# Landing two quarters of the first modulation's weights in empty weight slots, and taking the first products one stage later

## The chip, the core and the metric

The kernel runs on one core of a Trainium2 chip. The time is the device's, in microseconds (us), from the start of the program to its end; the kernel before took 2618.04 us (median of three runs, 2617.7 to 2619.2). A core has TensorE (PE in the profile; PEld is its loading of the stationary operand), VectorE (DVE), ScalarE (ACT), GpSimd (POOL) and SyncE (SP). Each works through its own list of instructions in the order in which the program gives them, and they wait for each other and for transfers by semaphores. SP issues nearly all transfers from the chip's memory (HBM) into SBUF; PSUM is what TensorE writes.

## The reference, cut to what matters

A diffusion block of two layers over 256 rows of x and 256 of a context, then four layers over x. The change touches the beginning of the first layer alone, for `i = 0`:

```python
m_lat = (jax.nn.silu(c) @ ada_w[i] + ada_b[i])[:, None, :]
m_ctx = jax.nn.silu(c_ctx) @ ada_w[i] + ada_b[i]
sh1, sc1, g1, sh2, sc2, g2 = jnp.split(m_lat, 6, axis=-1)
h  = _rms(x, norm1_g[i]) * (1.0 + sc1) + sh1          # (1, 256, 1024)
hc = _rms(y, norm1_g[i]) * (1.0 + csc1) + csh1        # the context, the same way
# first lines of the even mixer: h @ ev_w_in, hc @ ev_w_in, 1280 columns:
# 512 of the Fourier part (f0, f1), 512 of q (q0, q1), 256 of k and v (kv)
```

So a vector of 1024 is multiplied by 1024 x 2048 weights (shift and scale, 8 MB), x and the context are normalised, scaled and shifted by the result, and these are multiplied by 1024 x 1280 weights (five units of 256 columns, 1 MB each).

## The kernel before, in words

**Precision.** Products with large weights are done as three matmuls of a short form: a weight unit `wraw` of 128 x 2048 f32 is split into a high part `whi` (a cast on ScalarE) and a low part `wlo` (a subtraction on VectorE), each in two halves of 1024; activations are split the same way into `hTh` and `hTl`. One product (`mm3`) is whi x hTh, wlo x hTh, whi x hTl. The modulation's weights are not split: `wraw` is multiplied by `silu_c` as it is.

**Weights.** The class `Weights` keeps one list of units in the order of use. `load` (L249) takes the next unit, a free raw buffer of three (`RAW_BUFS`), and lets SP issue the transfer; the modulation's units are issued in two pieces of 512 KB (L258), others in one of 1 MB (L260). `split` (L286) takes a free weight slot, a pair of `hi` and `lo` buffers, and emits the two casts and two subtractions. At the start there are three slots, "0", "1" and "2". `pump` (L265) does both as far as buffers allow, and is called whenever a unit is done with (`done`, L322) and at each poll. Whether a split is emitted at such a point is decided by the class `Pace`, a running account of when each engine would be free. The order of instructions is so fixed when the program is built; which splits, softmax steps and products stand before which follows from that account, and everything in the first layer's attention is placed by it too. Its numbers are its own; the times in this text are the trace's.

**The first modulation.** `Even.plan` (L1631) puts the 2048 columns into four quarters p = 0..3 of 256 columns of the shift and 256 of the scale, two units (h = 0, 1) of 1 MB each, with the first three units of the mixer behind the first three quarters: ada0, f0, ada1, kv, ada2, q0, ada3. `Even.start` (L1649) loops over p: the two units are multiplied by `silu_c` into a bank (`acc<-wraw,silu_c`); VectorE copies the bank out (`rows`); TensorE transposes the four pieces (`acc<-consts,rows`); VectorE reduces them (`red`) and makes shift `sh` and scale `sc`; both engines apply them to columns 2p and 2p + 1 of the transposed x (`hf<-xT,sh,sc`); a cast and a subtraction give `hTh` and `hTl` of these columns. Products are put between: those of f0 up to column 2p ahead of the transposition of the rows, those of kv and q0 behind it (`products(1, 2 * p)`, `products(p, 2 * p)`). The context is loaded and normalised (`bins[1].A`) in the stage p = 2. After the loop the context's first 128 rows are transposed (`acc<-consts,hn`), the last products of f0, kv and q0 are taken, and the results are copied out by ScalarE (`f<-mm`, `kv<-mm`, `q<-acc`). The second 128 rows' transposition (`mm<-consts,hn`) writes banks that were f0's.

Almost all instructions pass one helper, so they have the line L67; they are told apart by the names of their tiles.

Of the kernel before, what the change touches and what calls it, by code (L numbers as in the profile page):

```python
# [7 lines left out]
F32 = mybir.dt.float32  # L8
F32R = mybir.dt.float32r
# [6 lines left out]
KD = 8  # L16
# [40 lines left out]
class Engine:  # L57


    def __init__(self, eng, name, pace):  # L60
        self.eng, self.name, self.pace = eng, name, pace
# [150 lines left out]
class Weights:  # L212
# [5 lines left out]
    def __init__(self, K):  # L218
        self.K = K
        self.units = []  # L220
        self.index = {}
        self.dma_n = self.split_n = 0
        self.at = -1
        self.part = None
        self.finished = set()
        self.raw = {}
        self.hl = {}
        self.raw_free = list(range(RAW_BUFS))
        self.slots = []
        self.closing = set()  # L230

# [14 lines left out]
    def check_closed(self, name):  # L246
        assert all(x[2][1] != name for x in self.hl.values()), name

    def load(self):  # L249
        key, src, raw, _ = self.units[self.dma_n]  # L250
        nc = self.K.nc
        r = self.raw_free.pop(0)
        t = self.K.raw_p.tile([128, 2048], F32, tag=f"raw{r}", name="wraw")
        shp = src.shape
        if len(shp) == 4:
            v = t.rearrange("p (a b c) -> p a b c", a=shp[1], b=shp[2])
            for i in range(shp[2]):
                nc.sync.dma_start(out=v[:, :, i, :], in_=src[:, :, i, :])  # L258
        else:
            nc.sync.dma_start(out=t if len(shp) == 2 else t.rearrange("p (a b) -> p a b", a=shp[1]), in_=src)  # L260
        nc.loaded(t)
        self.raw[self.dma_n] = (t, r)
        self.dma_n += 1

    def pump(self, force=None):  # L265
        now = self.K.nc.now
        while True:
            moved = False
            if self.dma_n < len(self.units) and self.raw_free:
                self.load()  # L270
                moved = True
            if self.split_n < self.dma_n:
                u = self.split_n
                ahead = sum(not x[2] for x in self.units[self.at + 1:u])
                lead = SPLIT_LEAD[min(ahead, len(SPLIT_LEAD) - 1)]
                idle = max(now["act"], now["dve"]) <= self.K.t + lead and (ahead < HOLD_AHEAD or not self.K.soon())
                if self.units[u][2]:
                    self.split_n += 1
                    moved = True
                elif force is not None and u <= force or \  # L280
                        idle and self.K.nc.ready(self.raw[u][0]) <= max(self.K.t, now["act"]) + 200:
                    moved = self.split(u)
            if not moved:
                return
# [37 lines left out]
    def done(self, key, need=3):  # L322
        u = self.index[key]
        self.finished.add(u)
        if self.units[u][2]:
            self.raw_free.append(self.raw.pop(u)[1])
        if u in self.hl:
            slot = self.hl.pop(u)[2]
            if slot[1] not in self.closing:
                self.slots.append(slot)  # L330
        self.K.poll(need)


class Kernel:
# [52 lines left out]

    @staticmethod
    def slot(pool):
        return lambda tag: pool.tile([128, 2048 + 128], F32R, tag=tag, name="w" + tag[:2])  # L390

    def close_ext(self, n):
        if n in self.ext:
# [803 lines left out]
class Conv:  # L1197
    PADL = 15
    W = 288
# [423 lines left out]
class Even:  # L1623
# [7 lines left out]
    def plan(self):  # L1631
        K = self.K
        w = K.a["ada_w"][0]
        for p in range(4):
            for h in range(2):
                src = w[h * 512:h * 512 + 512, 0:2048].rearrange("(k p) (x n) -> p k x n", p=128, x=2)
                K.W.add(("ada0", p, h), src[:, :, :, p * 256:p * 256 + 256], raw=True)
            if p < 3:
                K.add_in(("e", self.UNITS[p][0]), K.a["ev_w_in"][0], self.UNITS[p][1], "nat")
        for n, c in self.UNITS[3:]:  # L1640
            K.add_in(("e", n), K.a["ev_w_in"][0], c, "nat")
        for g in (1, 2):
            for k in range(KD):
                K.ada_plan(0, g, k)
        for e in range(2):
            for i in range(4):
                K.add_down(("e", "d", e, i), K.a["ev_w_out"][0], i)

    def start(self, bins):  # L1649


        K, nc, W = self.K, self.K.nc, self.K.W
# [3 lines left out]
        hT = bins[0].hT = K.new_hT()  # L1656
# [1 line left out]
        K.mod[0, "sh1"], K.mod[0, "sc1"] = sh, sc  # L1658
        bias, gain = K.sp("ab").rearrange("p (x k) -> p x k", x=2), K.sp("n1")
        far = K.acct()  # L1660
        units, done, xT = [], [0, 0, 0], []
        for p in range(4):
            for h in range(2):
                w = W.get(("ada0", p, h))
                for j in range(4):
                    K.mm32(far[0][32 * j:32 * j + 32, :], K.silu_c[:, 4 * h + j, :], w[:, j * 512:j * 512 + 512], h == 0, h == 1,
                           share=4, tile_position=(0, 32 * j))
                W.done(("ada0", p, h))
            if p == 2:
                for t in range(2):  # L1670
                    nc.sync.dma_start(out=K.y[t], in_=K.a["ctx"][0, t * 128:t * 128 + 128, :])
                    nc.loaded(K.y[t])
                    bins[1].A(t)
            rows = K.ada_p.tile([128, 512], F32, tag="r0", name="rows")
            nc.vector.tensor_copy(rows, far[0])
            if p == 0:
                for t in range(2):
                    ps = K.transposed(bins[0].h[t])
                    xT.append(K.h1_p.tile([128, KD, 128], F32, tag="h1", name="xT", bufs=2))
                    for b in range(2):  # L1680
                        (nc.vector.tensor_copy if b else nc.scalar.copy)(xT[t][:, 4 * b:4 * b + 4, :], ps[b])
                two = K.acct()
                units = [[K.mmt([128, 256]) for _ in range(2)] for _ in range(2)] + [[x[:, 0:256] for x in two]]

            def products(n, k1):
                for i in range(n):
                    wh, wl = W.get(("e", self.UNITS[i][0]))
                    for t in range(2):
                        s = slice(t * 128, t * 128 + 128)
                        for k in range(done[i], k1):  # L1690
                            K.mm3(units[i][t], hT[0][:, k, s], hT[1][:, k, s], wh[:, k, :], wl[:, k, :], k == 0, k == KD - 1)
                    done[i] = k1
                    K.tick()
            if p:
                products(1, 2 * p)
            tp = far[1].rearrange("p (c n) -> p c n", c=4)
            for c in range(4):
                K.tr(tp[:, c, :], rows[:, c * 128:c * 128 + 128])
            red = K.ada_p.tile([128, 2, 2, 2], F32, tag="red", name="red", bufs=2)
            nc.vector.tensor_reduce(out=red, in_=tp.rearrange("p c (j r) -> p c r j", j=4)[:, :, 0:2, :], axis=mybir.AxisListType.X, op=ALU.add)  # L1700
            if p:
                products(p, 2 * p)
            f = slice(2 * p, 2 * p + 2)
            bc = lambda x: x[:, f].unsqueeze(2).to_broadcast([128, 2, 2])
            out = lambda x: x[:, :, f].rearrange("p e k -> p k e")
            nc.vector.tensor_tensor(out=out(sh), in0=red[:, 0], in1=bc(bias[:, 0]), op=ALU.add)
            nc.vector.tensor_tensor(out=red[:, 1], in0=red[:, 1], in1=bc(bias[:, 1]), op=ALU.add)
            nc.vector.scalar_tensor_tensor(out=out(sc), in0=red[:, 1], scalar=1.0, in1=bc(gain), op0=ALU.add, op1=ALU.mult)
            hf = (K.s4_p if p % 2 else K.h1_p).tile([128, 2, 256], F32, tag=("hf", "junk")[p % 2], name="hf", bufs=1)
            for k in (2 * p, 2 * p + 1):  # L1710
                x = k - 2 * p
                nc.scalar.activation(out=hf[:, x, 0:128], in_=xT[0][:, k, :], func=AF.Identity, scale=sc[:, 0, k:k + 1], bias=sh[:, 0, k:k + 1])
                nc.vector.tensor_scalar(out=hf[:, x, 128:256], in0=xT[1][:, k, :], scalar1=sc[:, 0, k:k + 1], scalar2=sh[:, 0, k:k + 1],
                                        op0=ALU.mult, op1=ALU.add)
            K.split_psum(hT[0][:, f, :], hT[1][:, f, :], hf)

        bins[1].finish(0)
        halves = K.transposed(bins[1].h[0], [x.rearrange("p (j c) -> p j c", j=4) for x in far])
        products(3, KD)
        bins[1].hT = K.new_hT(1)  # L1720
        K.transpose_h(halves, bins[1].hT, 0, bins[1].cols())
        bins[1].put_off(1)
# [671 lines left out]
```

## Time and profile before

| | |
|---|---|
| median of three runs | 2618.04 us (2617.7 to 2619.2) |
| the profiled execution | 2618.8 us, span 2617.0 us |
| TensorE busy | 2539.5 us, 97% of the span |
| VectorE, ScalarE busy | 1494.3 us (57%), 1201.8 us (46%) |
| transfers | 453.59 MB, mean 173 GB/s |
| granted TensorE clock, mean | 0.993 of full speed |

The granted clock is a share of 2.4 GHz; 0.5 is 1.2 GHz. Engines work at the same time, so busy times don't add up to the span. In a timeline a row is a group of like instructions: start, busy time, engine, line, operation, output<-input, count, and in brackets the idle time of the engine ahead of it and what ended that.

### The profile page before, as it was taken

The page shows a single profiled execution, that of the slowest core. Times are in us where ns is not written, and L with a number is a line of the kernel's source. Part 1 is how long each engine was busy: PE and PEld are TensorE (multiplying, and loading weights), DVE is VectorE, ACT ScalarE, POOL GpSimd, SP SyncE. Part 2 cuts the span into 40 slices and gives each one's busy share as a digit, 9 for nine tenths or more (in the row PEclk, how much of TensorE's full clock was granted, in tenths as well). Part 3 has the DMA queues.
Part 4 walks back from the last instruction along what each step waited for, and adds up shares of the span by engine and source line. Part 5 has one row for each costly group of instructions (what it writes and reads, how often), then busy time and mean ns, then how long its engine had stood idle before and what let it go on. Part 6 is the DMA issues. An engine that isn't in the chain of part 4 may idle for free.

```text
span 2617.0 us, 43849 instructions
## 1 busy us (share of the span) xinstructions
PE 2539.5 (97%) x18444; PEld 2264.1 (87%) x18444; DVE 1494.3 (57%) x2420; ACT 1201.8 (46%) x2050; POOL 117.2 (4%) x168
## 2 busy tenths in 40 slices
PE   7889999999999999999999899999999999999998
PEld 5648877788877999999998689989998999999998
DVE  4477333366666655756555465555655655755644
ACT  4555222245444544545444354445554544544542
POOL 1100000001221000000000000000000000000000
PEclk9999999999999999999999999999999999999999
DMA  7355454545453655554655726544343654554652
GB/s 266 119 204 193 144 196 162 190 149 165 128 175 109 227 194 202 177 177 146 216 197 175 219 97 210 194 168 155 130 145 105 217 193 167 182 201 145 211 193 88
DMA packets 320741, 453.59 MB, mean 173 GB/s; under 512 B 20760, under 2 KB 281112, under 8 KB 315424
## 3 DMA queue, kind: packets, MB, share of 16 engines
q1 hardware_dynamic: 315552, 434.63, 49.9%
q0 software_dynamic: 4128, 14.11, 1.5%
q8 instruction: 145, 2.38, 0.4%
q10 hardware_dynamic: 864, 2.05, 0.2%
q14 instruction: 52, 0.43, 0.0%
HBM read 448.48 MB, written 2.28 MB: 172 GB/s over the span
## 4 chain that ended last, share of the span: by engine, by line
PE 84%; DVE 7%; DMA 4%; ACT 3%; issue 1%; SPq 1%; POOL 1%; POOLq 0%; DVEq 0%; ACTq 0%
PE mm L67 61%; PE acc L67 23%; DVE wlo L67 2%; DMA u<-up 1%; DMA wraw<-ada_w 1%; DVE sm L67 1%; DVE hTl L67 1%; DVE hn L67 1%; POOL ny L67 1%; ACT whi L67 1%; ACT jk L67 1%; ACT sm L67 0%; ACT hTh L67 0%; DMA wraw<-od_w_in 0%; SPq L1991 0%
## 5 line engine op out<-in xcount | busy, mean ns | idle before, releaser
L67 DVE TENSOR_TENSOR wlo<-wraw,whi 128x1024 fp32r<-128x1024 f32 x592 | 700.5, 1223 | 371.3 <-ACT whi L67 370.2
L67 ACT CAST whi<-wraw 128x1024 fp32r<-128x1024 f32 x592 | 592.7, 1048 | 311.3 <-issue 172.4
L67 PE MATMUL mm<-hTh,whi 128*128 128x256 f32 (+1 forms) x1840 | 543.1, 295 | 1.8 <-ACT hTh L67 1.8
L67 PE MATMUL mm<-hTl,whi 128*128 128x256 f32 (+1 forms) x1840 | 541.6, 294 | 0.3 <-DVE hTl L67 0.3
L67 PE MATMUL mm<-hTh,wlo 128*128 128x256 f32 (+1 forms) x1840 | 541.7, 294 | 0.0
L67 PE MATMUL mm<-whi,hTh 128*128 128x256 f32 x1616 | 464.5, 287 | 5.1 <-ACT hTh L67 3.2
L67 PE MATMUL mm<-whi,hTl 128*128 128x256 f32 x1616 | 455.2, 282 | 5.9 <-DVE hTl L67 5.9
L67 PE MATMUL mm<-wlo,hTh 128*128 128x256 f32 x1616 | 456.2, 282 | 0.9 <-DVE wlo L67 0.9
L67 PEld LDWEIGHTS mm<-hTh,whi 128*128 128x128 f32 x1840 | 346.1, 188 | 15.8 <-ACT hTh L67 2.0
L67 PEld LDWEIGHTS mm<-hTl,whi 128*128 128x128 f32 x1840 | 346.2, 188 | 13.1 <-DVE hTl L67 0.5
L67 PEld LDWEIGHTS mm<-hTh,wlo 128*128 128x128 f32 x1840 | 346.1, 188 | 11.2
L67 PEld LDWEIGHTS mm<-whi,hTh 128*128 128x128 f32 x1616 | 305.5, 189 | 23.1 <-issue 9.7
L67 PEld LDWEIGHTS mm<-whi,hTl 128*128 128x128 f32 x1616 | 307.7, 190 | 8.0 <-DVE hTl L67 8.0
L67 PEld LDWEIGHTS mm<-wlo,hTh 128*128 128x128 f32 x1616 | 306.5, 190 | 1.6 <-DVE wlo L67 1.1
L67 PE MATMUL acc<-whi,ckh 128*128 128x512 f32 x664 | 261.4, 394 | 0.0
L67 PE MATMUL acc<-whi,ckl 128*128 128x512 f32 x664 | 258.6, 390 | 0.6 <-DVE ckl L67 0.6
L67 PE MATMUL acc<-wlo,ckh 128*128 128x512 f32 x664 | 259.1, 390 | 0.0
L67 PE MATMUL mm<-hTh 128*128 128x256 f32 x656 | 184.6, 281 | 0.5 <-ACT hTh L67 0.5
L67 PE MATMUL mm<-hTh,hTl 128*128 128x256 f32 x656 | 182.9, 279 | 0.4 <-DVE hTl L67 0.4
L67 PE MATMUL mm<-hTl,hTh 128*128 128x256 f32 x656 | 182.9, 279 | 0.0
L67 DVE TENSOR_TENSOR hTl<-wraw,hTh 128x1024 fp32r<-128x1024 f32 x116 | 138.1, 1222 | 61.8 <-ACT hTh L67 60.8
L67 DVE TENSOR_TENSOR sg<-sg,mm 128x512 f32<-128x512 f32 (+1 forms) x67 | 40.2, 600 | 225.1 <-PE mm L67 222.3
(247 smaller groups left out, 3324.0 us busy)
## 6 DMA issues: line engine op xcount, KB each, us to landing
wraw<-ffn_w_in SPq DMA_DIRECT2D x88, 1024.0 KB, 5.0
wraw<-ret_w_in SPq DMA_DIRECT2D x48, 1024.0 KB, 5.0
wraw<-ffn_w_out SPq DMA_DIRECT2D x44, 1024.0 KB, 4.8
wraw<-ada_w SPq DMA_DIRECT2D x40, 1024.0 KB, 6.3
wraw<-attn_w_in SPq DMA_DIRECT2D x36, 1024.0 KB, 4.8
wraw<-ffn_w_down SPq DMA_DIRECT2D x33, 1024.0 KB, 4.9
wraw<-ffn_w_gate SPq DMA_DIRECT2D x22, 1024.0 KB, 5.2
wraw<-ffn_w_up SPq DMA_DIRECT2D x22, 1024.0 KB, 5.2
```

Source lines behind the costliest of these rows:

```text
L67: r = f(*args, **kw)
```

## The change

The loader and the stage loop of `Even.start` are changed. `lend` takes a weight slot off the free list and gives its `hi` buffer to one unit and its `lo` buffer to another; `load` then puts these units there and needs no raw buffer; `done` returns the slot once both are used. The two units of quarter 1 get slot "1", those of quarter 2 get slot "2". The list of units becomes ada0, f0, ada1, ada2, kv, ada3, q0. In `start` the loop is turned: quarter p + 1 is multiplied behind the scaling of quarter p, and f0's products up to column 2p + 2 stand behind it; kv's first products come in the stage p = 2, q0's after the loop; the context is normalised after the loop, and its first transposition stands behind f0's and kv's last products. f0's split is asked for ahead of the transposition of x.

```diff
+    def lend(self, name, keys):
+        slot = next(x for x in self.slots if x[1] == name)
+        self.slots.remove(slot)
+        left = set(keys)
+        for w, key in zip(("hi", "lo"), keys):
+            self.guests[self.index[key]] = w, slot, left
+
     def load(self):
         key, src, raw, _ = self.units[self.dma_n]
         nc = self.K.nc
-        r = self.raw_free.pop(0)
-        t = self.K.raw_p.tile([128, 2048], F32, tag=f"raw{r}", name="wraw")
+        r = None
+        if self.dma_n in self.guests:
+            w, slot, _ = self.guests[self.dma_n]
+            t = slot[0](w + slot[1], F32)[:, 0:2048]
+        else:
+            r = self.raw_free.pop(0)
+            t = self.K.raw_p.tile([128, 2048], F32, tag=f"raw{r}", name="wraw")
...
-            if p < 3:
-                K.add_in(("e", self.UNITS[p][0]), K.a["ev_w_in"][0], self.UNITS[p][1], "nat")
+            if p != 1:
+                n, c = self.UNITS[(p + 1) // 2]
+                K.add_in(("e", n), K.a["ev_w_in"][0], c, "nat")
+        for p in (1, 2):
+            K.W.lend(str(p), [("ada0", p, h) for h in range(2)])
...
+        rows = modulation(0)
+        W.get(("e", self.UNITS[0][0]))
+        for t in range(2):
+            ps = K.transposed(bins[0].h[t])
...
+        for p in range(4):
             tp = far[1].rearrange("p (c n) -> p c n", c=4)
             for c in range(4):
                 K.tr(tp[:, c, :], rows[:, c * 128:c * 128 + 128])
...
             K.split_psum(hT[0][:, f, :], hT[1][:, f, :], hf)
+            if p == 2:
+                products(1, 4)
+                for t in range(2):
+                    nc.sync.dma_start(out=K.y[t], in_=K.a["ctx"][0, t * 128:t * 128 + 128, :])
+                    nc.loaded(K.y[t])
+            if p < 3:
+                rows = modulation(p + 1)
+                products(0, 2 * p + 2)
+        products(1, 6)
+        products(2, 6)
+        for t in range(2):
+            bins[1].A(t)
+        for i in range(2):
+            products(i, KD)
 
         bins[1].finish(0)
         halves = K.transposed(bins[1].h[0], [x.rearrange("p (j c) -> p j c", j=4) for x in far])
-        products(3, KD)
+        products(2, KD)
```

What the program's lists say of it, at three places. First SP, from the program's beginning, before and then changed (ev_w_in is f0, kv, q0 in this order; a row ending in x4 is two units of the modulation):

```order
L258 DMA wraw<-ada_w 128x4x256 x4
L260 DMA wraw<-ev_w_in 128x8x256
L258 DMA wraw<-ada_w 128x4x256 x4
L260 DMA wraw<-ev_w_in 128x8x256
L258 DMA wraw<-ada_w 128x4x256 x4
L260 DMA wraw<-ev_w_in 128x8x256
L258 DMA wraw<-ada_w 128x4x256 x4
```
```order
L272 DMA wraw<-ada_w 128x4x256 x4
L274 DMA wraw<-ev_w_in 128x8x256
L272 DMA whi<-ada_w 128x4x256 x2
L272 DMA wlo<-ada_w 128x4x256 x2
L272 DMA whi<-ada_w 128x4x256 x2
L272 DMA wlo<-ada_w 128x4x256 x2
L274 DMA wraw<-ev_w_in 128x8x256
L272 DMA wraw<-ada_w 128x4x256 x4
L274 DMA wraw<-ev_w_in 128x8x256
```

kv moved behind the quarters 1 and 2, and q0 behind quarter 3. Second VectorE, around the copy of quarter 1's rows, before and then changed; wraw_117 is f0 in both kernels, wraw_202 in the changed one is kv:

```order
L67 TENSOR_TENSOR hTl_86<-hf_243,hTh_85 128x512
L67 TENSOR_TENSOR wlo_257<-wraw_117,whi_256 128x1024 x2
L67 COPY rows_272<-acc_184 128x512
L67 TENSOR_REDUCE red_290<-acc_185 128x8
L67 TENSOR_TENSOR sh1_182<-red_290,small_88 128x2x2
```
```order
L67 TENSOR_TENSOR hTl_86<-hf_263,hTh_85 128x512
L67 TENSOR_TENSOR wlo_279<-wraw_202,whi_278 128x1024 x2
L67 COPY rows_286<-acc_196 128x512
L67 TENSOR_REDUCE red_304<-acc_197 128x8
L67 TENSOR_TENSOR sh1_194<-red_304,small_88 128x2x2
```

The place ahead of the copy is now kv's split; f0's moved to the front, ahead of the copies of xT. Third TensorE, around the context's first transposition, before and then changed (`mm` are the banks of f0 and kv, `acc` those of q0):

```order
L67 MATMUL acc<-whi,hTh 128x256
L67 MATMUL acc<-wlo,hTh 128x256
L67 MATMUL acc<-whi,hTl 128x256
L67 MATMUL acc<-consts,hn 128x128 x8
L67 MATMUL mm<-whi,hTh 128x256
L67 MATMUL mm<-wlo,hTh 128x256
L67 MATMUL mm<-whi,hTl 128x256
```
```order
L67 MATMUL mm<-whi,hTh 128x256
L67 MATMUL mm<-wlo,hTh 128x256
L67 MATMUL mm<-whi,hTl 128x256
L67 MATMUL acc<-consts,hn 128x128 x8
L67 MATMUL acc<-whi,hTh 128x256
L67 MATMUL acc<-wlo,hTh 128x256
L67 MATMUL acc<-whi,hTl 128x256
```

The 24 products of f0 and kv that stood behind the transposition now stand ahead of it; q0's twelve are left behind it, and then `mm<-consts,hn`.

## Rows read from the trace of the kernel before

**Rows 1.** The page, busy time and share of the span.
```profile
PE 2539.5 (97%) x18444; PEld 2264.1 (87%) x18444; DVE 1494.3 (57%) x2420; ACT 1201.8 (46%) x2050; POOL 117.2 (4%) x168
```
**Rows 2.** Waits of PE, first 75 us: us in total, times, longest.
```profile
PE acc L67 <- DMA wraw<-ada_w: 17.7, 6, 10.0
```
**Rows 3.** Stretches: length, busy of five engines, granted clock, DMA share, GB/s.
```profile
12.00:20.00 8.00, 7.17 (x36) 4.46 (x36) 4.40 (x12) 2.25 (x5) 0.56 (x1) 1.00 1.09 385
20.00:33.00 13.00, 5.60 (x32) 2.38 (x32) 8.16 (x15) 6.42 (x10) 0.00 (x0) 0.84 0.77 248
33.00:38.00 5.00, 4.84 (x22) 3.21 (x23) 0.69 (x1) 0.00 (x0) 0.00 (x0) 0.50 1.02 351
38.80:44.00 5.20, 4.61 (x41) 3.11 (x39) 3.84 (x9) 3.39 (x5) 0.00 (x0) 0.98 1.06 401
```
**Rows 4.** Timeline of PE, the modulation's products and transpositions.
```profile
20.83 1.06 PE L67 MATMUL acc<-wraw,silu_c 128*32 128x512 f32 x8 [0.98 <-DMA wraw<-ada_w]
...
25.17 0.66 PE L67 MATMUL acc<-consts,rows 128*128 128x128 f32 x4 [0.17 <-DVE rows L67]
...
29.54 1.94 PE L67 MATMUL acc<-wraw,silu_c 128*32 128x512 f32 x8 [3.71 <-DMA wraw<-ada_w]
...
33.16 1.93 PE L67 MATMUL acc<-wraw,silu_c 128*32 128x512 f32 x8 [1.69 <-DMA wraw<-ada_w]
...
35.40 0.41 PE L67 MATMUL mm<-wlo,hTh 128*128 128x256 f32 x1
...
37.53 0.41 PE L67 MATMUL mm<-whi,hTl 128*128 128x256 f32 x1
...
37.75 1.05 PE L67 MATMUL acc<-consts,rows 128*128 128x128 f32 x4
...
43.35 1.06 PE L67 MATMUL acc<-wraw,silu_c 128*32 128x512 f32 x8 [0.59 <-DMA wraw<-ada_w]
```
**Rows 5.** Timeline of ACT and DVE between these, stages p = 1 and 2.
```profile
21.08 1.99 ACT L67 CAST whi<-wraw 128x1024 fp32r<-128x1024 f32 x2
...
22.15 2.36 DVE L67 TENSOR_TENSOR wlo<-wraw,whi 128x1024 fp32r<-128x1024 f32 x2 [0.26 <-ACT whi L67]
...
24.43 0.68 DVE L67 COPY rows<-acc 128x512 f32<-128x512 f32 x1
...
38.84 0.19 DVE L67 TENSOR_REDUCE red<-acc 128x8 f32<-128x32 f32 x1 [3.00 <-PE acc L67]
...
39.54 0.88 ACT L67 ACTIVATE hf<-xT,sh,sc 128x128 f32<-128x128 f32 x2 [9.56 <-DVE sc L67]
...
40.45 0.62 ACT L67 CAST hTh<-hf 128x512 fp32r<-128x512 f32 x1
...
41.10 0.69 DVE L67 TENSOR_TENSOR hTl<-hf,hTh 128x512 fp32r<-128x512 f32 x1 [0.96 <-ACT hTh L67]
```
**Rows 6.** Timelines of PE, ACT and DVE around the context's transpositions.
```profile
51.96 1.04 PE L67 MATMUL acc<-consts,hn 128*128 128x128 f32 x8
52.75 0.37 PE L67 MATMUL mm<-whi,hTh 128*128 128x256 f32 x1
...
57.08 1.03 PE L67 MATMUL mm<-consts,hn 128*128 128x128 f32 x8
...
44.55 0.63 ACT L67 ACTIVATE jk<-y 128x512 bf16<-128x512 f32 x1 [1.59 <-DMA y<-ctx]
...
55.19 0.64 ACT L67 COPY f<-mm 128x256 f32<-128x256 f32 x2
55.71 0.66 ACT L67 COPY kv<-mm 128x256 f32<-128x256 f32 x2
...
57.71 1.51 ACT L67 ACTIVATE hf<-mm,sh,sc 128x128 f32<-128x128 f32 x4
...
46.95 0.75 DVE L67 TENSOR_SCALAR hn<-y,ny 128x1024 f32<-128x1024 f32 x1 [0.73 <-POOL ny L67]
```
**Rows 7.** Timeline of PE in the attention, its longest wait.
```profile
117.78 3.51 PE L67 MATMUL mm<-cs,f 128*128 128x512 f32 x4 [4.96 <-ACT sm L67]
```

More of the change, by code (lines that the diff above doesn't have):

```diff
@@ L228, in __init__ @@
         self.raw_free = list(range(RAW_BUFS))
+        self.guests = {}
         self.slots = []
@@ L268, in pump @@
             moved = False
-            if self.dma_n < len(self.units) and self.raw_free:
+            if self.dma_n < len(self.units) and (self.raw_free or self.dma_n in self.guests):
                 self.load()
@@ L324, in done @@
         self.finished.add(u)
-        if self.units[u][2]:
+        if u in self.guests:
+            self.raw.pop(u)
+            _, slot, left = self.guests[u]
+            left.remove(key)
+            if not left:
+                self.slots.append(slot)
+        elif self.units[u][2]:
             self.raw_free.append(self.raw.pop(u)[1])
@@ L389, in slot @@
     def slot(pool):
-        return lambda tag: pool.tile([128, 2048 + 128], F32R, tag=tag, name="w" + tag[:2])
+        return lambda tag, dt=F32R: pool.tile([128, 2048 + 128], dt, tag=tag, name="w" + tag[:2])
     def close_ext(self, n):
@@ L1660, in start, with modulation @@
         far = K.acct()
-        units, done, xT = [], [0, 0, 0], []
-        for p in range(4):
+        units, done, xT, rows = [], [0, 0, 0], [], None
+        def modulation(p):
             for h in range(2):
@@ L1668, in start @@
                 W.done(("ada0", p, h))
[L1669 to L1673, printed above, removed]
             rows = K.ada_p.tile([128, 512], F32, tag="r0", name="rows")
             nc.vector.tensor_copy(rows, far[0])
[L1676 to L1695, printed above, removed]
+            return rows
@@ new lines, in products @@
+        def products(i, k1):
+            wh, wl = W.get(("e", self.UNITS[i][0]))
+            for t in range(2):
+                s = slice(t * 128, t * 128 + 128)
+                for k in range(done[i], k1):
+                    K.mm3(units[i][t], hT[0][:, k, s], hT[1][:, k, s], wh[:, k, :], wl[:, k, :], k == 0, k == KD - 1)
+            done[i] = k1
+            K.tick()
+        rows = modulation(0)
+        W.get(("e", self.UNITS[0][0]))
+        for t in range(2):
+            ps = K.transposed(bins[0].h[t])
+            xT.append(K.h1_p.tile([128, KD, 128], F32, tag="h1", name="xT", bufs=2))
+            for b in range(2):
+                (nc.vector.tensor_copy if b else nc.scalar.copy)(xT[t][:, 4 * b:4 * b + 4, :], ps[b])
@@ L1696, in start @@
+        two = K.acct()
+        units = [[K.mmt([128, 256]) for _ in range(2)] for _ in range(2)] + [[x[:, 0:256] for x in two]]
+        for p in range(4):
             tp = far[1].rearrange("p (c n) -> p c n", c=4)
@@ L1700, in start @@
             nc.vector.tensor_reduce(out=red, in_=tp.rearrange("p c (j r) -> p c r j", j=4)[:, :, 0:2, :], axis=mybir.AxisListType.X, op=ALU.add)
-            if p:
-                products(p, 2 * p)
             f = slice(2 * p, 2 * p + 2)
@@ L1715, in start @@
             K.split_psum(hT[0][:, f, :], hT[1][:, f, :], hf)
+            if p == 2:
[8 more added lines that the diff above has]
+        products(2, 6)
+        for t in range(2):
+            bins[1].A(t)
+        for i in range(2):
+            products(i, KD)
         bins[1].finish(0)
         halves = K.transposed(bins[1].h[0], [x.rearrange("p (j c) -> p j c", j=4) for x in far])
-        products(3, KD)
+        products(2, KD)
         bins[1].hT = K.new_hT(1)
```

## The prediction

> **What bounds the kernel now.** I read the page's busy shares first: TensorE is busy 97% of the span [rows 1], so the change can only pay where TensorE waits. The list of waits for the first 75 us comes next. There the reader is to see one line that outweighs all others: 17.7 us in six waits for the transfer of ada_w, the modulation's weights [rows 2]. The stretches of the same time say why: the transfers run at 385 GB/s from 12 to 20 us, but at 248 GB/s from 20 to 33 us [rows 3]. The loader has three raw buffers there and stands still until one is free. The timeline last: quarter 1's second unit lets TensorE go on at 20.83, quarter 2's units at 29.54 and 33.16, quarter 3's last one at 43.35 [rows 4]. (Modulation p below is the product of quarter p.) From there on TensorE has no gap to 58 us and beyond, so what the change is worth is how much earlier or later TensorE reaches the same work at 57.08, the second transposition of the context's rows [rows 6].
>
> **What goes.** Eight pieces of half a megabyte now land in weight slots 1 and 2, which stand empty, so SP issues modulations 1 and 2 right behind f0 without waiting for a raw buffer. At 385 GB/s one megabyte (1.049e6 bytes) takes 2.72 us. Up to the last byte of modulation 1 the queue holds the same bytes in the same order in both kernels, so that lands at 20.83 as before [rows 4]. Behind it come 2 MB of modulation 2, 1 MB of kv and 2 MB of modulation 3: they land at 26.3, 29.0 and 34.4. The last one came at 43.35. By this alone TensorE could be 8.9 us earlier.
>
> **What is late next: VectorE.** The changed order puts the split of kv (two casts on ScalarE, two subtractions on VectorE) ahead of the copy of modulation 1's rows on VectorE. Before, it was f0's split that stood there, and its cast at 21.08 waited for no transfer. That a copy waits for what stands ahead of it is to be seen in the trace: modulation 1's products ended at 20.83 + 1.06 = 21.89, and the copy began at 24.43, as the subtractions that began at 22.15 and took 2.36 ended [rows 4, 5]. In the changed kernel kv lands at 29.0 and the same group runs from there. From the first cast at 21.08 to the transposition of the rows at 25.17 were 4.09 us [rows 4, 5]; so this transposition comes at 33.1 instead of 25.17. Modulation 2's weights, in by 26.3, lie idle until then. TensorE does modulation 2 right behind that transposition (two groups of 1.94 us at the low clock [rows 4]), beside the chain below.
>
> Two smaller edits lie under that pause and cost nothing while it stands: f0's split now comes ahead of the copies of the transposed x, by two casts and two subtractions, and SP issues eight more pieces in a row, while it has nothing else to do. Without the pause the first would delay the first products by about 1 us (two subtractions of 2.36 us from f0's landing, less what ScalarE and VectorE waited for there).
>
> The bounds on kv's landing: at 401 GB/s, the best stretch nearby [rows 3], 28.7; with one stall of SP like the loss from 20 to 33 us (13 us x (385 - 248)/385 = 4.6), 33.6. I take 29.0, since the queue has 4 MB waiting by then and the 12 to 20 us stretch was fed in the same half-megabyte pieces.
>
> The Trainium skill, "DMA: Bandwidth & Descriptors", section "Measured (HBM→SBUF, 128 partitions, SWDGE, issued from GpSimd)", speaks against small pieces: transfers should be batched to a megabyte or more, and one of a megabyte is listed at 341 GB/s. As an estimate from that page, the 3 MB behind modulation 1 would take 9.2 us instead of 8.2, and the sum below would grow by 1.0. The trace disagrees for pieces that queue behind each other: half-megabyte ones ran at 385 GB/s [rows 3], and the measurement decides.
>
> **The chain from there.** TensorE's clock was at 0.50 of full speed from 33 to 38 us, after a pause from 25.8 to 29.5 and another to 33.16 [rows 3, 4]: that is 1.2 GHz. In the changed kernel TensorE ends f0's first products near 25, as before, and then pauses some 8 us, so I take the low level for what follows. At that level transposition to reduction takes 38.84 - 37.75 = 1.09, reduction to hf 0.70, hf to hTh 0.91, hTh to hTl 0.65, and hTl itself 0.69 [rows 4, 5]: from 33.1, hTl is ready at 37.15. One matmul of a split product takes (37.53 - 35.40)/10 = 0.213 at 1.2 GHz and (57.08 - 52.75)/36 = 0.120 at 2.4 GHz [rows 4, 6].
> - f0, two columns, two row halves, three matmuls each: twelve, ten of them behind hTl: to 39.3 at the low level.
> - Transposition of modulation 2's rows 0.85; then 24 matmuls of kv; then modulation 3, two groups of 1.06.
> - When does the clock rise? Before, it rose between 38.0 and 38.8 [rows 3], at most 5.6 us after TensorE went on without a break at 33.16. At the earliest it rises at 38.7 again: then f0's matmuls end at 39.1, the transposition at 39.6, kv's at 42.5, modulation 3 at 44.6. Counted from 37.1 it rises at 42.7: transposition to 40.2, 11.7 matmuls at 0.213, 12.3 at 0.120, modulation 3 at 46.3. Before, it ended at 43.35 + 1.06 = 44.41 [rows 4].
>
> So the end of the modulations, the point that should have come 8.9 us earlier, comes 0.2 to 1.9 us later; I take 1.0. q0's split stands ahead of modulation 3's rows in the same way, but q0, one megabyte behind modulation 3, has landed by 38; its group ends within 0.3 us of the modulation's products, worth 0.1.
>
> **A second new wait.** The context's first transposition now stands behind f0's and kv's last products, and only q0's twelve matmuls are left between it and the second transposition, where 36 were. The second one writes the banks that f0's results lie in, and ScalarE copies these out after it has made hf and hTh from the first: from 51.96, the start of the first, to the end of f's copies at 55.19 + 0.64 is 3.87 us [rows 6]. The cover is now 0.79 (52.75 - 51.96) + 12 x 0.120 = 2.2 us. So TensorE waits 1.7 us, where before it came 5.12 us after (57.08) and didn't wait. Behind it, f0's products for the context's second half need the second hTh; ScalarE began on it 57.71 - 57.08 = 0.63 after that transposition; now kv's two copies (0.66 us [rows 6]) and q's two of the same shape stand in between, 1.3 us. So 0 to 0.7; I take 0.2, since the 24 matmuls of the first half lie in front. The context's squares and scaling (44.55 to 46.95 + 0.75, 3.15 us) start after hTh of modulation 3 and end before its transposition, since 72 matmuls (8.6 us) lie beside them: nothing.
>
> **The attention behind it** (100 to 215 us) is emitted by the planner in another order, with the same instructions. The trace doesn't show this order. Its largest wait is 4.96 us, ended by ScalarE at 117.78 [rows 7]; the bounds are that wait gone (-5.0) and one more like it (+5.0). I take 0: the same instructions stand there, and the order in front of that largest wait is unchanged on TensorE and VectorE. Everything after is unchanged instruction by instruction, and TensorE has work there, so a shift passes to the end.
>
> **Sum:** 1.0 + 0.1 + 1.7 + 0.2 + 0 = +3.0 us. The profiled execution took 2618.8 (span 2617.0 and 1.8 around it), 0.8 above the median of the three runs, 2618.04. On the median: 2621.0. The measurement can tell 0.2%, 5.2 us, from no change; +3.0 is within that.
>
> **Rivals.**
> - The prefetch pays in full. The wait for kv doesn't hold the rows (VectorE does the copy first, or kv is in by 21 us): modulation 3 ends at 34.4 + 1.06 = 35.5, 8.9 us earlier, and 2.0 us go back in the second new wait: -6.9, 2611. For it: 17.7 us of waits for exactly these weights. Against it: the copy at 24.43 stood behind the subtractions [rows 5], and kv can't land before 28.7. The Trainium skill, "TensorE: Matmul & The Clock Gate", section "Architectural detail: the array is 16× 32×32, not 1× 128×128", says that VectorE's and ScalarE's queues keep strict order; by it this rival is shut, and the trace agrees at 24.43.
> - The attention's new order costs one wait more like the 4.96 us at 117.78 [rows 7], where TensorE's scores need banks that ScalarE's softmax has not read: +3.0 + 5.0 = 2626. It decides against the forecast as soon as the waits from 100 to 215 us grow by over 2.2 us. For it: ScalarE now has a copy of fm between the first two steps of softmax, and that waits for TensorE. Against it: in the same place the softmax of the context, whose banks TensorE waits for, comes first now.
> - The start loses 3 us and the attention's order gives them back: 2618.
>
> **Chances.** Forecast 0.50, prefetch in full 0.12, attention worse 0.23, attention better 0.15. Faster by over 0.2%: the first rival and a little of the last, 0.14. Slower by over 0.2%: the second rival and the upper end of the forecast's own terms (1.9 + 0.3 + 1.7 + 0.7 = 4.6, and anything late with kv), 0.27. Within: 0.59. The forecast's own range is 2619.5 to 2623; with 8 of 10 it reaches to 2612.5 below and 2627 above.
>
> **What would show it.** VectorE's copy of modulation 1's rows begins near 32.4, as kv's second subtraction ends; TensorE has nothing from about 25 to 33; no wait for ada_w is left after 21 us; modulation 3's products end between 44.6 and 46.3; a wait of 1 to 2.5 us, ended by ScalarE's copy of f, stands before the second transposition of the context, which ends near 60. I am wrong if TensorE's products of f0 for modulation 1 run before 30 us, if that transposition starts before 57, or if the shift at 60 us and the one at the end differ by over 3 us, which would be the attention's.

## The result, and the profile after

The changed kernel takes 2632.97 us (median of four runs, 2631.26 to 2637.17) where the kernel before takes 2617.87 (2617.11 to 2619.2) beside it: a ratio of 1.0054, 95% interval 1.0042 to 1.0066, about 14 us slower. The profiled execution took 2631.26, with a span of 2629.5 us, 12.5 longer than before.

TensorE's busy time rose by 4.6 us only (2539.5 in [rows 1]), so most of the loss is waiting, and the 4.6 are the same matmuls at a lower clock (mean 0.990, before 0.993). The page, busy time:

```profile
PE 2544.1 (97%) x18444; PEld 2266.0 (86%) x18444; DVE 1495.8 (57%) x2420; ACT 1201.7 (46%) x2050; POOL 117.2 (4%) x168
```

**The start.** First the waits of PE in the first 75 us (us in total, times, longest) and the stretches that answer to [rows 3]:

```profile
PE acc L67 <- DMA wraw<-ada_w: 10.7, 2, 10.0
PE acc L67 <- DVE rows L67: 8.7, 1, 8.7
PE mm L67 <- ACT f L67: 1.2, 1, 1.2
PE acc L67 <- DMA wlo<-ada_w: 0.8, 1, 0.8
```
```profile
20.00:33.00 13.00, 3.03 (x21) 1.74 (x21) 4.66 (x9) 3.49 (x5) 0.00 (x0) 0.85 1.09 385
33.00:38.00 5.00, 5.00 (x29) 2.46 (x30) 2.49 (x8) 1.50 (x3) 0.00 (x0) 0.71 1.02 344
```

The transfers no longer stand still (385 GB/s from 20 to 33 us where [rows 3] has 248), and of the 17.7 us of waits for ada_w [rows 2] 6.2 are gone: 10.7 are left, and 0.8 under the name of the slot's buffer (`wlo<-ada_w`). In their place stands one wait of 8.7 us for VectorE's copy of the rows. The timeline shows why:

```profile
28.89 1.99 ACT L67 CAST whi<-wraw 128x1024 fp32r<-128x1024 f32 x2 [6.81 <-DMA wraw<-ev_w_in]
...
29.97 2.36 DVE L67 TENSOR_TENSOR wlo<-wraw,whi 128x1024 fp32r<-128x1024 f32 x2 [7.16 <-ACT whi L67]
...
32.25 0.68 DVE L67 COPY rows<-acc 128x512 f32<-128x512 f32 x1
...
32.99 1.12 PE L67 MATMUL acc<-consts,rows 128*128 128x128 f32 x4 [8.68 <-DVE rows L67]
34.03 1.94 PE L67 MATMUL acc<-whi,silu_c 128*32 128x512 f32 x8
35.74 1.11 PE L67 MATMUL acc<-wlo,silu_c 128*32 128x512 f32 x8
...
41.78 1.92 PE L67 MATMUL acc<-wraw,silu_c 128*32 128x512 f32 x16
...
57.91 1.09 PE L67 MATMUL mm<-consts,hn 128*128 128x128 f32 x8 [1.19 <-ACT f L67]
```

ScalarE waits for kv's transfer, VectorE for ScalarE, and the copy stands behind both. Modulation 3 ends at 43.70, where before it ended at 44.41 [rows 4]. At the attention's first product (`mm<-cs,f`) the shift is 100.47 - 99.31 = +1.2 us.

**The attention and its end.** The other 11.3 us of the 12.5 arise behind that point. The waits of PE from 100 to 300 us, before and after:

```profile
PE mm L67 <- ACT sm L67: 5.7, 3, 5.0
PE mm L67 <- DVE rows L67: 3.9, 5, 1.2
...
PE mm L67 <- ACT pt L67: 1.8, 4, 0.7
PE mm L67 <- ACT fm L67: 0.9, 3, 0.3
```
```profile
PE mm L67 <- ACT pt L67: 4.0, 4, 1.1
PE mm L67 <- DMA wraw<-ada_w: 3.3, 2, 1.9
PE mm L67 <- ACT sm L67: 3.1, 3, 2.6
PE mm L67 <- ACT fm L67: 2.8, 2, 2.6
PE mm L67 <- DVE hn L67: 2.7, 1, 2.7
...
PE acc L67 <- DVE wlo L67: 1.2, 2, 1.0
```

Over all rows of the two answers the waits grow from 15.4 to 21.7 us, +6.3. The wait of 4.96 us for the softmax [rows 7], from which the prediction took its bounds, is down to 2.64. Stretches of that time (the last three numbers are granted clock, DMA share, GB/s), before and after:

```profile
160.00:180.00 20.00, 16.86 (x132) 7.99 (x129) 15.73 (x52) 8.72 (x29) 1.77 (x3) 1.00 0.80 276
200.00:300.00 100.00, 97.85 (x639) 87.67 (x638) 56.28 (x85) 43.03 (x71) 4.71 (x8) 0.98 0.49 170
```
```profile
160.00:180.00 20.00, 18.08 (x122) 9.50 (x120) 14.97 (x51) 10.39 (x34) 1.76 (x3) 0.91 0.19 67
200.00:300.00 100.00, 93.35 (x566) 81.75 (x567) 58.29 (x86) 45.52 (x72) 6.94 (x12) 0.92 0.54 187
```

From 160 to 180 us the transfers run at 67 GB/s instead of 276, and from 200 to 300 us TensorE's clock is lower and TensorE is idle for 6.65 us instead of 2.15. What stands between is in TensorE's timeline at the end of the attention, before and after. `mm<-wraw,silu_c` are the multiplications of the first layer's gate modulations: sixteen units of raw weights, each of which holds a raw buffer until TensorE has multiplied it. I call them the gate units.

```profile
185.91 1.07 PE L67 MATMUL mm<-wraw,silu_c 128*32 128x512 f32 x8
...
196.47 1.09 PE L67 MATMUL mm<-consts,rows 128*128 128x128 f32 x8
```
```profile
198.38 1.06 PE L67 MATMUL mm<-wraw,silu_c 128*32 128x512 f32 x8 [1.89 <-DMA wraw<-ada_w]
...
200.82 1.94 PE L67 MATMUL mm<-wraw,silu_c 128*32 128x512 f32 x8 [1.37 <-DMA wraw<-ada_w]
202.69 1.98 PE L67 MATMUL mm<-consts,rows 128*128 128x128 f32 x8
...
206.13 0.80 PE L67 MATMUL acc<-wlo,hTh 128*128 128x512 f32 x1 [1.04 <-DVE wlo L67]
```

The last gate unit came at 185.91, in the midst of the attention, and now comes at 200.82, behind its last step, with TensorE waiting for its transfer; the first product of the out-projection then waits for its own `wlo`. By 180 us 13 of the sixteen units were done, and now 8. That the loader waits for them is to be seen on SP, in the order of the units: it issues the last gate units and then the out-projection's weights (`ev_w_out`), here from their first issue to 215 us, before and after:

```profile
183.88 28.48 SPq L260 DMA_DIRECT2D wraw<-ev_w_out  x8
```
```profile
196.54 17.50 SPq L274 DMA_DIRECT2D wraw<-ev_w_out  x6
```

The shift is +6.2 at 202.69 and +13.8 at the first wait for `hTh` of the next block (262.86 before, 276.67 after). So 5.0 us of the 11.3 arise within the attention, and 7.6 in the out-projections behind it (1.3 are regained later). Of the 7.6, waits for `wlo` and `hn` that before does not have there are 3.9; the other 3.7 are left to the clock. From 200 to 210 us, before and after:

```profile
200.00:210.00 10.00, 10.00 (x46) 8.29 (x45) 2.95 (x4) 3.49 (x4) 0.00 (x0) 1.00 0.62 247
```
```profile
200.00:210.00 10.00, 8.14 (x26) 5.08 (x27) 5.99 (x10) 3.99 (x4) 2.23 (x4) 0.50 0.99 354
```

### The profile page after: what moved, and what is told of

Same layout as the page of the kernel before. It is cut to its first block, busy times and chain, and to the rows that moved or that the text cites. A ratio compares the mean times of both kernels' runs of the same rounds, so it can differ in the third digit from the quotient of the medians.

```text
span 2629.5 us, 43841 instructions
## 1 busy us (share of the span) xinstructions
PE 2544.1 (97%) x18444; PEld 2266.0 (86%) x18444; DVE 1495.8 (57%) x2420; ACT 1201.7 (46%) x2050; POOL 117.2 (4%) x168
## 4 chain that ended last, share of the span: by engine, by line
PE 84%; DVE 7%; DMA 4%; ACT 3%; issue 1%; POOL 1%; SPq 1%; POOLq 0%; DVEq 0%; ACTq 0%
PE mm L67 61%; PE acc L67 23%; DVE wlo L67 2%; DVE sm L67 1%; DVE hTl L67 1%; DVE hn L67 1%; POOL ny L67 1%; DMA u<-up 1%; DMA wraw<-ada_w 1%; ACT jk L67 1%; ACT sm L67 1%; ACT whi L67 1%; DMA taps<-u 0%; DMA wraw<-od_w_in 0%; ACT hTh L67 0%
```

## The experiments

Theory 1: the loss is not the new start's but the order that the account `Pace` chose for the instructions behind it; 1a: in that order, the place of the gate units. Theory 2: the change itself costs it. The table has medians and ratios to the kernel before on the same chip; us is (ratio - 1) x 2618. For the kernel after it is +14.1.

| run | median | ratio, 95% | us |
|---|---|---|---|
| e1 after, before's order behind the start | 2619.77 | 1.0008 (0.9999 to 1.0017) | +2.1 |
| e2 before, after's order behind the start | 2627.33 | 1.0037 (1.0024 to 1.0049) | +9.7 |
| e3 as e1, splits held back | 2610.89 | 0.9974 (0.9963 to 0.9985) | -6.8 |
| e4 as e3, context's transposition as before | 2613.33 | 0.9979 (0.9971 to 0.9988) | -5.5 |
| e5 after, gate units at before's steps | 2621.21 | 1.0014 (1.0006 to 1.0023) | +3.7 |
| e6 before, gate units at after's steps | 2631.33 | 1.0057 (1.0045 to 1.0069) | +14.9 |
| e7 as e3, the account's own order | 2629.40 | 1.0040 (1.0028 to 1.0052) | +10.5 |
| e8 as e7, gate units at before's steps | 2619.43 | 1.0008 (0.9999 to 1.0016) | +2.1 |
| e9 after, two filler entries per turn | 2624.04 | 1.0028 (1.0016 to 1.0039) | +7.3 |
| e10 before, two filler entries per turn | 2619.28 | 1.0005 (0.9996 to 1.0014) | +1.3 |
| e11 as e3, two filler entries per turn | 2612.69 | 0.9985 (0.9977 to 0.9994) | -3.9 |
| e12 as e11, the account's own order | 2618.79 | 1.0003 (0.9994 to 1.0012) | +0.8 |

**e1 and e2: the order against the change.** The account's clocks and tile times are overwritten at one point (e2: the same two edits to the kernel before, with after's values):

```diff
             units = self.start(bins)
+            settle(K)
...
+def settle(K):
...
+    nc.now = {'pe': 62351, 'act': 60473, 'dve': 61196, 'pool': 53256}
```

> The kernel after with one addition: where the start ends, the planner's account (clocks of its engines, times of the tiles) is set to the values that it has there in the kernel before. The start is the changed one; behind it every engine has its instructions in the order of the kernel before. Nothing is left out of the computation. Theory 1, the loss is the order that the account chose behind the start: only the start's own price of +1.2 us is left (the first product of the attention, mm<-cs,f, 99.31 before, 100.47 after), so 2618 to 2620 us against 2617.9, and the attention's end (first PE wait for hTh) at about 264 instead of 276.7. Theory 2, the loss is the change itself (turned slots, q0 and the raw pieces later, their DMAs): 2630 us or more, as the kernel after.

> The kernel before with one addition: where the start ends, the planner's account is set to the values that it has there in the kernel after. The start is that of before; behind it every engine has its instructions in the order of the kernel after. Nothing is left out. Theory 1: the order alone costs about 12 to 13 us, so 2629 to 2632 us; the first PE wait for hTh at about 275 instead of 262.9. Theory 2: 2617 to 2619 us, as before.

In the traces the lists of TensorE, VectorE and ScalarE behind the start are before's in e1 and after's in e2, instruction by instruction. Theory 2 falls: the change with before's order costs 2.1 us, which is not clear of zero, and after's order costs 9.7 without the change. The 9.7 is less than expected, and the two don't quite add up to 14.1; the first wait for `hTh` comes at 267.18 in e1, 3 us later than expected, and at 272.72 in e2. In e2 the trace shows the same pattern as after: the last gate unit at 199.12, the `hn` wait of 2.65 at 269.82:

```profile
199.12 1.42 PE L67 MATMUL mm<-wraw,silu_c 128*32 128x512 f32 x8 [2.98 <-DMA wraw<-ada_w]
...
269.82 1.09 PE L67 MATMUL mm<-consts,hn 128*128 128x128 f32 x8 [2.65 <-DVE hn L67]
```

**e3 and e4: what the start could have given.** e3 keeps kv's and q0's splits off the lists until the rows copies stand there; e4 moves the context's transposition forward again.

```diff
-                        idle and self.K.nc.ready(self.raw[u][0]) <= max(self.K.t, now["act"]) + 200:
+                        idle and self.units[u][0] not in self.hold and self.K.nc.ready(self.raw[u][0]) <= max(self.K.t, now["act"]) + 200:
...
+        W.hold = {("e", "kv"), ("e", "q0")}
         rows = modulation(0)
...
                 rows = modulation(p + 1)
+                if p:
+                    W.get(("e", self.UNITS[p][0]))
```

> As the first (changed start, order of before behind it), and the splits of kv and q0 into whi and wlo are held back until the rows copies of modulations 1 and 2 stand in DVE's queue, so that the rows copy no longer stands behind the wlo split that waits for kv's DMA (wlo 29.97, rows copy 32.25 in the kernel after). Theory 1 with the queue as the start's price: rows copy at about 24.5, PE's 8.7 us wait for rows gone, end of modulation 3 at about 37 to 38 instead of 43.7, 2612 to 2614 us. Rival: modulation 3 waits for its own weights (DMA) anyway, or what is gained is given back at the first products: 2618 to 2620 us, as the first.

e4 besides:

```diff
-        for i in range(2):
-            products(i, KD)
-
         bins[1].finish(0)
...
-        products(2, KD)
+        for i in range(3):
+            products(i, KD)
         bins[1].hT = K.new_hT(1)
```

> As the third, and the first transposition of the context stands again ahead of the last products of f0 and kv, as in before, so that the second transposition's wait for f on ACT (1.19 us, mm<-consts,hn at 57.91 in the kernel after) is covered. Theory: that wait goes, another 1.2 to 1.9 us, 2610 to 2612 us. Rival: PE waits for kv's hTl or the context's rsqrt at the same place instead: 2612 to 2614 us, as the third.

In e3 the copy stands at 22.73, TensorE goes on at 24.15 where it stood until 32.99, and modulation 3, the last to come, ends at 36.76:

```profile
22.73 0.68 DVE L67 COPY rows<-acc 128x512 f32<-128x512 f32 x1
...
24.15 0.60 PE L67 MATMUL acc<-consts,rows 128*128 128x128 f32 x4
...
35.70 1.06 PE L67 MATMUL acc<-wraw,silu_c 128*32 128x512 f32 x8 [0.47 <-DMA wraw<-ada_w]
```

So the queue was the start's price: 8.9 us lie between e1 and e3, whose lists behind the start are the same, and in the traces 7.4 of them stand at 60 us. e3 beats both kernels, by 6.8 us and by about 21, and the 2612 to 2614 expected of it by a little. In e4 the wait for f goes and one of 2.79 us for the context's own rows comes in its place, as the rival said:

```profile
47.89 1.09 PE L67 MATMUL acc<-consts,hn 128*128 128x128 f32 x8 [2.79 <-DVE hn L67]
```

**e5 to e8: the place of the gate units.** The attention's loop takes one entry of a list of filler work (Fourier products, then gate units) each time that the poll has nothing due. Counted in steps (tasks run and scores begun), the last entry comes after 82 steps in before and after 90 in after. These runs take each entry after a given number of steps:

```diff
+AT = [6, 16, 16, 16, 16, 16, 16, 17, 21, 28, 28, 31, 39, 39, 42, 50, 50, 53, 61, 61, 61, 64, 70, 71, 72, 81, 81, 82]
...
+            def between():
+                while fill and K.ran >= AT[-len(fill)]:
+                    fill.pop(0)()
...
                 K.poll()
-                if fill:
-                    fill.pop(0)()
-                elif K.t == before:
+                if K.t == before:
                     K.run(K.tasks[0])
```

> The kernel after, its account left as it is, but the list of the attention's filler work (the first Fourier products and, at its end, the multiplications of the gate modulations, mm<-wraw,silu_c) is taken from after the same number of attention steps as in the kernel before (the last of 28 entries after 82 steps, in after itself after 90). The out-projections then stand in the order of before too. Nothing is left out. Theory 1a, the late multiplications (last at 200.82 us in after, 185.91 before) hold the raw weight buffers, and the weights behind them come late: 2618 to 2622 us, the 3.3 us of waits for wraw<-ada_w and the 1 us for wlo before the out-projection gone. Theory 1b, it is another part of the order (the fm copy ahead of the softmax, 2.6 us twice; the pt waits, 1.1 us three times): 2625 to 2630 us.

> The kernel before with the filler list taken from after the numbers of attention steps of the kernel after (the multiplications of the gate modulations come late); the out-projections keep the order of before. Nothing is left out. Theory 1a: the part of the loss that had arisen up to the out-projections in the second run, 4 to 6 us, so 2621 to 2624 us; the other 4 us or so of that run's 9.5 belong to the out-projections' order (the hn wait of 2.65 us at 269.82). Theory 1b: 2617 to 2619 us.

e5 brings after from +14.1 to +3.7; e6 takes before to +14.9, with before's start and before's order in the out-projections. Stretch and timeline of e5, then of e6:

```profile
160.00:180.00 20.00, 17.17 (x149) 8.91 (x148) 14.83 (x45) 9.47 (x31) 1.76 (x3) 1.00 0.60 215
```
```profile
186.82 1.07 PE L67 MATMUL mm<-wraw,silu_c 128*32 128x512 f32 x8 [1.38 <-DVE ae L67]
```
```profile
160.00:180.00 20.00, 17.45 (x138) 10.39 (x139) 13.51 (x49) 11.23 (x37) 1.76 (x3) 1.00 0.20 68
```
```profile
205.69 1.07 PE L67 MATMUL mm<-wraw,silu_c 128*32 128x512 f32 x8 [1.46 <-DMA wraw<-ada_w]
...
210.66 0.80 PE L67 MATMUL acc<-whi,hTh 128*128 128x512 f32 x1 [2.45 <-ACT whi L67]
```

With the units late the transfers fall to 68 GB/s and TensorE waits for raw weights and then for a split, before's start or not; with them early they run at 215 and the waits from 100 to 300 us sum to 16.0, near before's 15.4. Theory 1a stands. (e6's trace is of its slowest execution, 5.8 us above its median.) e6 exceeds its 4 to 6 us, so the out-projections' other order, to which I had given 4 us of e2's loss, is not needed for the loss. The list moves as one, Fourier products and units, so these runs don't part the units from the `fm` waits (2.8 us after): what they show is the price of the list's place, and that the units are the dear part of it is read from the transfers and waits above.

> The third kernel without setting the account: the splits of kv and q0 are held back, and the order behind the start is what the account itself chooses. It takes the filler work after the same numbers of attention steps as the kernel after. Theory 1a: the start's gain of about 7 us (2610.9 against 2617.8) stays and the late units' loss of 6 to 13 us comes on top, 2617 to 2624 us. Theory 1b or the start alone deciding: 2610 to 2613 us.

> The seventh kernel with the filler list taken after the numbers of attention steps of the kernel before. Theory 1a: as the third kernel, 2609 to 2613 us. Theory 1b: little better than the seventh, 2617 us or more.

With e3's start, too, the early list is worth 8.4 us. But e7 is slower than the 2617 to 2624 expected, and e8 is 8.9 us behind e3, which theory 1a doesn't explain: by its own expectation e8's time is that of theory 1b. At 190 us the two are level (`mm<-consts,rows` at 190.39 in e8 and 190.56 in e3). In the traces, which end 11.0 apart, e8 loses 3.1 by 261 us, and the largest part, 5.8, between 835 and 860 us, where it waits for a split that e3 has done:

```profile
850.66 0.38 PE L67 MATMUL mm<-whi,hTh 128*128 128x256 f32 x1 [1.41 <-ACT whi L67]
851.92 0.38 PE L67 MATMUL mm<-wlo,hTh 128*128 128x256 f32 x1 [0.88 <-DVE wlo L67]
```

That cast of `whi` starts at 842.01 in e3 and at 849.57 in e8: a second place where the account, far behind the edit, chose another order. The two waits are 2.3 of the 5.8 us; no run sets this place alone.

**e9 to e12: a rule in place of a table.** Two entries of the filler list per turn:

```diff
                 if fill:
                     fill.pop(0)()
+                    if fill:
+                        fill.pop(0)()
                 elif K.t == before:
```

> The kernel after, with one rule changed: in the attention's loop two entries of the filler list are taken per turn and not one, so that the multiplications of the gate modulations come earlier, whatever the account says. No setting of the account. Behind the attention all engines have the order of the kernel before. Nothing is left out. Theory 1a (late multiplications make the loss): the loss of the attention goes, the start's 2 to 3 us stay, 2618 to 2622 us. Rival: taken this early, the filler work pushes the attention's own steps back and the loss comes back in another place, 2625 us or more.

> The kernel before with the same one rule (two filler entries per turn). If earlier multiplications still paid, 2612 to 2616 us; if before already has them early enough, 2617 to 2619 us; if filler work pushes the attention back, 2620 us or more. I take the second.

> The third kernel (splits held back, account set to before's where the start ends) with two filler entries per turn. As the third, 2609 to 2613 us, if the kernel before has the multiplications early enough; lower by what the tenth gains otherwise.

> The same without setting the account: splits held back, two filler entries per turn, all else chosen by the account. If the multiplications' place is all that matters: as the eleventh, within 2 us. If the second place found in the eighth run (waits for whi and wlo near 850 us, where the account chose another order and the kernel lost 9 us against the third) is real, 2617 to 2621 us.

e9 halves the loss, but misses its 2618 to 2622. Its units are not late: the last stands at 186.26, with 72 matmuls between it and the end of the attention, as many as in before. What it has instead are two waits for `pt`, the transposed softmax that the next products need:

```profile
189.79 2.35 DVE L67 TENSOR_TENSOR wlo<-wraw,whi 128x1024 fp32r<-128x1024 f32 x2
...
192.06 0.68 DVE L67 COPY pt<-mm 128x512 f32<-128x512 f32 x1
...
192.80 1.98 PE L67 MATMUL mm<-pt,kv 128*64 128x128 f32 x16 [3.01 <-DVE pt L67]
...
197.93 3.88 ACT L67 CAST whi<-wraw 128x1024 fp32r<-128x1024 f32 x4
...
202.36 0.66 PE L67 MATMUL mm<-pt,kv 128*64 128x128 f32 x8 [2.95 <-ACT pt L67]
```

Each time the short copy of `pt` stands behind splits of the out-projection's weights, on VectorE behind two subtractions and on ScalarE behind four casts: the start's pattern again, here without a transfer that is waited for. So early units alone don't make a good order, and the place of the splits has a price of its own. e10 and e11 gain nothing over before and e3: before has the units early enough. e12's time is what I expected of the place at 850 us, but its trace has no such wait (the cast starts at 844.91, not late), and the same two `pt` waits near 190 us as e9. So the expectation was met by luck. The trace is of e12's fastest execution, 3.6 us under its median and only 0.9 longer than e11's; why e12 is 4.7 us behind e11 stays open.

## Why the prediction was wrong, point by point

- **What goes, and the chain of the start: right.** kv landed at 28.9 (29.0), the rows copy began at 32.25 (32.4), its transposition at 32.99 (33.1), TensorE had nothing from 24.3 to 33.0. The sentence of the Trainium skill that the prediction weighed, "DMA: Bandwidth & Descriptors", section "Measured (HBM→SBUF, 128 partitions, SWDGE, issued from GpSimd)" (341 GB/s for a megabyte), would have these transfers slower. The trace disagrees: the stretch from 20 to 33 us shows 385, and kv came at the time that 385 gives.
- **The end of the modulations:** said +0.2 to +1.9, measured -0.7 (43.70 against 44.41). The step was the clock: I let the low level last to 38.7 at the earliest, by a time that the rows give as the most that it can have lasted before. The stretch from 33 to 38 us has 0.71, so the clock rose inside it: the first eight matmuls of modulation 2 took 1.94 us, the second eight, from 35.74, 1.11.
- **The second new wait:** 1.7 said, 1.19 measured, at the place and with the releaser named. The trace puts the whole start at +1.2 and e1 at +2.1, against the sum's +3.0.
- **The attention: the step that failed.** "I take 0: the same instructions stand there, and the order in front of that largest wait is unchanged", with bounds of 5 us from one wait [rows 7]. It measured 11.3 us in the trace. That wait did shrink, and a wait of 2.6 us for ScalarE's copy of `fm`, which now stands ahead of softmax steps, took its place; the loss came in the main from another change of order, the gate units fifteen microseconds later, and from what hangs on them: raw buffers, hence the transfers, the splits of the out-projection and TensorE's clock. I had seen in the start that three raw buffers can stop the loader [rows 3], and did not ask the same question of the attention, where the same buffers wait for the same kind of instruction. The comparison of the lists would have shown the units' place before any run; the bound should have been what a stopped loader costs there, not one more softmax wait.
- "Everything after is unchanged instruction by instruction" was wrong too: TensorE's list differs as far as the out-projections and the next block's first products. But from 276.67 on the shift does pass to the end (+13.8 there, +12.5 at the end). The prediction's own sign of this step came: the shift at 60 us, +0.9, and the one at the end differ by far more than 3.
- **The rivals.** The second (the attention's new order costs more) was nearest. The waits from 100 to 215 us grew from 13.2 to 17.0, more than its 2.2; the copy of `fm` that it names does make TensorE wait; and its price, 5.0, is what arose within the attention. It missed the gate units and with them the 7.6 us in the out-projections, and it expected more of the softmax wait, which shrank; that its price fits is in part luck. The first (prefetch in full, -6.9, 2611, "VectorE does the copy first") is what e3 built, and it came out at -6.8, 2610.9: its condition, not its sum, was missing.

## What to carry to other kernels

Where a running account places instructions, an edit at the start changes decisions far behind it: compare the lists to the end, and read each moved instruction by what it holds (a buffer, a bank), not by its own duration. To tell an edit's own price from that of the order it causes, set the account back behind the edit, and set it so in the unchanged kernel as well. A split should not stand in an engine's list ahead of short work that another engine waits for: TensorE waited 8.7 us for it where the split waited for a transfer, and 3.0 in e9 where it didn't.

## What the runs showed of the hardware beyond that

The same list of instructions got different clocks. After and e1 have the same start, but from 33 to 38 us after was granted 0.71 (above) and e1 0.50, with 29 and 20 matmuls done in the 5 us:

```profile
33.00:38.00 5.00, 4.60 (x20) 1.31 (x20) 2.23 (x8) 1.50 (x3) 0.00 (x0) 0.50 1.01 335
```

Behind the start e2 and after have the same lists, shifted by 0.4 us against each other at 110 us and by 1.2 at 160, and were granted 1.00 and 0.91 (above) from 160 to 180 us. This is e2:

```profile
160.00:180.00 20.00, 16.46 (x128) 9.21 (x126) 16.23 (x59) 11.45 (x38) 1.76 (x3) 1.00 0.19 67
```

So the list of instructions alone does not fix the clock, nor what a pause of TensorE costs beyond its length: behind a pause of 8.7 us in both, modulation 2's second eight matmuls took 1.11 us in after and 1.94 in e1. What decides it is not shown. This may be where e1 and e2 fail to add up to the whole; no run tested it.
